# A diffusion backbone step on one core: the down projection's 512 columns as two matmuls of 256, the convolution's tokens divided at 384

## The chip, the cores and the metric

The kernel is one program on one core of a Trainium2 chip. The core has five engines with their own instruction queues: PE (TensorE, matrix products), DVE (VectorE), ACT (ScalarE), POOL (GpSimd) and SP (SyncE, which here only issues DMAs). A matmul has a *stationary* operand, which a weight load (PEld in the profile) puts into the array, and a *moving* operand, whose columns stream past it; the result is written to PSUM, an accumulator memory whose banks hold 512 f32 values in each of 128 partitions. The other working memory is SBUF.

The metric is the device time of one execution in microseconds. Three runs of the kernel before gave 771.39, 771.91 and 772.88 us; the median is 771.91 us.

Two words are used throughout. The *duration* of a matmul is what the profile lists for one instruction; its end is modelled, and durations of neighbouring matmuls overlap. The *pitch* is the time from the start of one matmul to the start of the next one; in a run without gaps the pitch is what a matmul costs.

## The reference

One layer of a hybrid backbone: 128 context tokens and 512 latent tokens, 1024 features each, everything in f32.

```
mod = silu(cond) @ w_ada + b_ada
sh1, sc1, g1, sh2, sc2, g2 = split(mod, 6)
h = rms(x, norm_mix) * (1 + sc1) + sh1
q, k, v, gb, gc, u = split(h @ w_in)              # 512, 128, 128, 512, 512, 512 columns
attn   = attention(rope(rms(q)), rope(rms(k)), v)  # latent: context keys + latent keys
y_conv = gb * conv3(gc * u)                        # 3 taps along the tokens
mix = concat(rms(attn), rms(y_conv)) @ w_out
x = x + g1 * mix
h2 = rms(x, norm_ffn) * (1 + sc2) + sh2
gate, up = split(h2 @ w_gate_up)                   # 2816 columns each
x = x + g2 * ((silu(gate) * up) @ w_down)          # 2816 x 1024
```

The change touches `gb`, `gc` and `u` (the convolution's three projections) and the last product with `w_down`.

## The kernel before, in words

**Split products.** Each f32 operand is split into a high part, rounded to the type fp32r, and a low part, the rest. A product is three matmuls: high by high, high by low, low by high. The helper `mm3` issues them (L155, L156, L157); the convolution has its own three lines (L678, L679, L680). ACT makes the high part of a weight block (L151) and DVE the low part (L152) out of a block `wf` that SP loads; the results are the tiles `wh` and `wl`.

**The stages.** The program goes through the first norm and the queries (to about 61 us of the span), keys and values (61 to 75), attention (75 to 256), the output projection (256 to 325) and then the SwiGLU network (325 to the end). PE's instructions stand in the order in which they are written (a manual schedule); those of DVE and ACT are mostly set by a scheduler with its own cost estimates, and DMAs go through SP's queue.

**Keys and values** (`kv_mm`) take a 128-token slice of `hH` or `hL` (the normed input, features by tokens, high and low) as stationary operand and 256 columns of `wh` or `wl` as moving operand, into the PSUM tile `pc`.

**The convolution** runs the other way: for each of 12 blocks (three projections by four groups of 128 channels) 128 columns of weights are stationary and tokens of `hH` and `hL` move. The 640 tokens are two chunks of 320, each its own accumulator `pc` of 8 contraction tiles by 3 matmuls = 24 matmuls. This is filler work for attention: the generator `conv_mm` yields after k = 2, after k = 5 and at the end, so a chunk is three steps of 9, 9 and 6 matmuls. In the text order of attention (`SEQ`) each `F1` runs one step between a unit's scores (S, L790), transposes (T, L816) and products with the values (O, L833). A finished chunk is evicted by ACT (`gc`, L692) or multiplied by DVE (`u` at L701, `gb` at L713); the table `PIECES` cuts the second chunk where latent and context tokens meet.

**The network** has 22 blocks of 128 hidden columns in four groups of 6, 6, 5 and 5. Gate and up products use moving operands of 320 tokens (half of them) and stationary weights. After each group, `down` multiplies its hidden columns with `w_down`: for both halves j of the 1024 output columns and each of the 5 token tiles, one accumulator `pf` of 512 columns (one PSUM bank) collects, for every hidden block f of the group, three matmuls: a 128-token slice of `gT[f]` (tiles `gH` and `gL`) is stationary and 512 columns of `wh` or `wl` move. In the very last half of the last group the last token tile is halved instead: two accumulators of 256 columns each (`halved`, the variable TL). When an accumulator is done, DVE multiplies it by g2 (L1230) and adds it to x (L1231); in the last group SP then stores it.

Of the kernel before, what the change touches and what calls it, by code (L numbers as in the profile page):

```python
# [15 lines left out]
P = 128  # L16
# [68 lines left out]
AHEAD = 3  # L85
# [6 lines left out]
def build(ctx, tc, x_prompt, x_sample, c, cache_k, cache_v, c_ctx, norm_mix, norm_ffn, w_ada, b_ada,  # L92
# [66 lines left out]
    def rstd_of(ss, n, scale, extra=None, tag="rs"):  # L159
        """(ss * scale + eps) ** -0.5 (times extra)"""  # L160
# [34 lines left out]
    def op_load(e):  # L195
        """one stationary operand of a gate and up block: a quarter of the block, or a sum of quarters"""
        f, name = e[0][1:]
# [120 lines left out]
    def ada1_load(k):  # L318
        """w_ada of feature tile k of the first norm's scale and shift"""
# [51 lines left out]
    # products with the two conditions: four contraction tiles at a time on the four column groups of the  # L371
    # array, each with its conditions in the first columns; the groups' sums are added by sel afterwards
# [12 lines left out]
    def vec_do():  # L385
# [3 lines left out]
        # (1 + b_sc) * norm for both norms  # L389
# [7 lines left out]
    def mod_evict(i, f0, n, ps_sc, ps_sh):  # L397
        """ps_*: [P, n, 2] sums without bias for features f0..f0+n tiles"""
# [35 lines left out]
    def xT_do(t):  # L434
        """the normed tokens of tile t, feature-major"""
# [144 lines left out]
    def head_norm(ps, nh, t, which):  # L580
        """rms over each head, gain, rotary; ps [P, nh*64] -> SBUF f32 [P, nh, 64]"""
# [71 lines left out]
    def q_turn(st):  # L653
        q = T("qT", (P, NH, P), F32R, QTB)
        for g in range(2):
            tp = PB((P, 4, P), F32R)
            for h in range(4):
# [9 lines left out]
    CH = [(0, 320), (320, 320)]  # L667
    # (chunk, columns of the chunk, token columns, columns of the padded row)
    PIECES = [(0, slice(0, 320), slice(0, 320), slice(1, 321)),
              (1, slice(0, 192), slice(320, 512), slice(321, 513)),  # L670
              (1, slice(192, 320), slice(512, 640), slice(515, 643))]

    def conv_mm(off, ct, out):
        wh, wl = W(("conv", off, ct))
        for c0, n in CH:
            acc = PB((P, 320), tag="c")
# [94 lines left out]
    def F(n=1):  # L771
        for _ in range(n):
            if used[0] < NFILL:
                next(filler)
                used[0] += 1

# [1 line left out]
    of = [None] * NT  # L778
    rA = [None] * NT
    qT = [None] * NT  # L780
# [535 lines left out]
```

## Time and profile before

| | |
|---|---|
| median of three runs | 771.91 us (771.39 to 772.88) |
| span of the profiled execution, first to last instruction | 771.6 us; no device time of that execution stands beside it, the median is 0.3 us above the span |
| mean granted clock of TensorE | 0.989 of full speed |
| PE busy | 744.2 us, 96% of the span |
| weight loads (PEld) busy | 669.2 us, 87% |
| DVE, ACT, POOL busy | 563.1 us (73%), 376.8 us (49%), 70.8 us (9%) |
| DMA | 84.53 MB, mean 110 GB/s |
| matmuls of 128x512 in the down projection | 3 x 215 |
| matmuls of 128x256 in its last halved tile | 3 x 10 |
| matmuls of 128x320 in the convolution | 3 x 192 |

How to read the rows: in the timeline a row is start in us, duration in us, engine, source line, operation, output <- inputs by the program's names, the shape and the count. In the table of groups a row is line, engine, operation, names, shape and count, then busy us and mean ns of one, then the engine's idle time before them and what ended it. A row of windows gives a stretch, its length, then each engine's busy us with its number of instructions.

### The profile page before, as it was taken

How to read it: one execution, taken by the hardware profiler on the slowest of the kernel's cores; microseconds unless marked ns; L12 is line 12 of the kernel's file. 1: busy time of each engine (PE TensorE's matmuls, PEld its weight loads, DVE VectorE, ACT ScalarE, POOL GpSimd, SP SyncE). 2: the span in 40 equal slices, each digit the busy share in tenths (PEclk: the TensorE clock that was granted, in tenths of full speed). 3: DMA queues.
4: the chain of work that ended last, by engine and by line, in shares of the span. 5: the costliest groups of instructions: out<-in, count | busy, mean ns of one | idle time of the engine just before them, and what ended most of it. 6: DMA issues, size and time to landing. Idle time of an engine off the chain costs nothing.

```text
span 771.6 us, 11961 instructions
## 1 busy us (share of the span) xinstructions
PE 744.2 (96%) x4580; PEld 669.2 (87%) x4580; DVE 563.1 (73%) x1033; ACT 376.8 (49%) x732; POOL 70.8 (9%) x97
## 2 busy tenths in 40 slices
PE   4999999999999999996999999999999999999997
PEld 3778988989999787886998789999889998899986
DVE  5566887675666799789778777984677866788653
ACT  5446676666665346875452125554125542255510
POOL 3105101011010330044100000000000000000000
PEclk9999999999999999999899999999999999999999
DMA  9984134424325433111134412233112231222312
GB/s 290 308 236 128 42 109 140 121 90 140 120 89 171 161 133 110 56 55 55 56 110 153 134 55 83 83 109 110 54 56 82 83 109 56 80 84 84 110 55 82
DMA packets 102350, 84.53 MB, mean 110 GB/s; under 512 B 4526, under 2 KB 82674, under 8 KB 102292
## 3 DMA queue, kind: packets, MB, share of 16 engines
q1 hardware_dynamic: 100980, 83.39, 35.0%
q8 instruction: 36, 0.59, 0.3%
q10 hardware_dynamic: 1056, 0.26, 0.2%
q0 software_dynamic: 256, 0.11, 0.1%
q14 instruction: 22, 0.18, 0.1%
HBM read 79.68 MB, written 2.75 MB: 107 GB/s over the span
## 4 chain that ended last, share of the span: by engine, by line
PE 83%; DVE 8%; ACT 3%; DMA 2%; issue 2%; SPq 2%; POOL 1%; ACTq 0%; POOLq 0%
PE pf L155 17%; PE pf L157 17%; PE pf L156 17%; PE pc L678 3%; PE pc L679 3%; PE pc L680 3%; PE ps L155 3%; PE ps L156 3%; PE ps L157 3%; PE po L833 2%; PE ps L790 2%; PE pt L816 2%; PE pc L380 2%; DMA af<-in_w_ada_dram 2%; DVE wl L152 1%
## 5 line engine op out<-in xcount | busy, mean ns | idle before, releaser
L151 ACT ACTIVATE wh<-wf 128x1024 fp32r<-128x1024 f32 (+1 forms) x76 | 64.1, 843 | 93.1 <-PE pf L157 63.2
L155 PE MATMUL pf<-wh,gH 128*128 128x512 f32 (+1 forms) x225 | 88.2, 392 | 0.0
L157 PE MATMUL pf<-wh,gL 128*128 128x512 f32 (+1 forms) x225 | 87.7, 390 | 0.0
L156 PE MATMUL pf<-wl,gH 128*128 128x512 f32 (+1 forms) x225 | 87.7, 390 | 0.0
L152 DVE TENSOR_TENSOR wl<-wf,wh 128x1024 fp32r<-128x1024 f32 (+1 forms) x42 | 49.4, 1176 | 27.8 <-ACT wh L151 24.9
L678 PE MATMUL pc<-hH,wh 128*128 128x320 f32 x192 | 61.7, 321 | 0.0
L679 PE MATMUL pc<-hL,wh 128*128 128x320 f32 x192 | 60.0, 312 | 0.0
L680 PE MATMUL pc<-hH,wl 128*128 128x320 f32 x192 | 59.9, 312 | 0.0
L155 PE MATMUL pf<-T,wh 128*128 128x320 f32 x160 | 50.1, 313 | 6.2 <-ACT p L1125 6.2
L155 PEld LDWEIGHTS pf<-wh,gH 128*128 128x128 f32 x225 | 42.3, 188 | 9.8 <-ACT wh L151 0.2
L157 PEld LDWEIGHTS pf<-wh,gL 128*128 128x128 f32 x225 | 42.3, 188 | 9.8
L156 PEld LDWEIGHTS pf<-wl,gH 128*128 128x128 f32 x225 | 42.3, 188 | 9.8 <-issue 0.2
L156 PE MATMUL pf<-T,wh 128*128 128x320 f32 x160 | 49.9, 312 | 0.0
L157 PE MATMUL pf<-T,wh 128*128 128x320 f32 x160 | 49.9, 312 | 0.0
L155 PE MATMUL pf<-T,wl 128*128 128x320 f32 x160 | 49.3, 308 | 0.0
L156 PE MATMUL pf<-T,wl 128*128 128x320 f32 x160 | 49.3, 308 | 0.0
L157 PE MATMUL pf<-T,wl 128*128 128x320 f32 x160 | 49.3, 308 | 0.0
L156 PE MATMUL pf<-B,wl 128*128 128x320 f32 x152 | 47.5, 313 | 0.3 <-DVE B L1020 0.3
L155 PE MATMUL pf<-B,wl 128*128 128x320 f32 x152 | 47.4, 312 | 0.0
L157 PE MATMUL pf<-B,wl 128*128 128x320 f32 x152 | 47.2, 310 | 0.0
L1230 DVE TENSOR_TENSOR dm<-pf,g 128x512 f32<-128x512 f32 (+1 forms) x41 | 27.7, 676 | 22.9 <-PE pf L157 22.9
L151 ACT ACTIVATE wl<-wf 128x512 fp32r<-128x512 f32 x34 | 21.4, 630 | 43.5 <-PE pf L156 36.8
(308 smaller groups left out, 2097.5 us busy)
## 6 DMA issues: line engine op xcount, KB each, us to landing
wf<-in_w_gate_up_dram SPq DMA_DIRECT2D x44, 512.0 KB, 3.8
aw<-in_w_ada_dram SPq DMA_DIRECT2D x24, 512.0 KB, 4.7
wf<-in_w_down_dram SPq DMA_DIRECT2D x20, 512.0 KB, 3.2
wf<-in_w_in_dram SPq DMA_DIRECT2D x18, 512.0 KB, 5.9
af<-in_w_ada_dram SPq DMA_DIRECT2D x32, 256.0 KB, 6.1
x<-in_x_sample_dram SPq DMA_DIRECT2D x8, 512.0 KB, 5.3
wf<-in_w_out_dram SPq DMA_DIRECT2D x8, 512.0 KB, 4.5
wf<-in_w_ada_dram SPq DMA_DIRECT2D x8, 512.0 KB, 3.8
```

The costliest lines, as they stand in the source:

```text
L151: act.activation(hi, src, AF.Copy)
L152: dve.tensor_tensor(lo, src, f32(hi), ALU.subtract)
L155: pe.matmul(out, lh, rh, start=start, stop=False, skip_group_check=more)
L156: pe.matmul(out, lh, rl, start=False, stop=False, skip_group_check=more)
L157: pe.matmul(out, ll, rh, start=False, stop=stop, skip_group_check=more)
L380: pe.matmul(out[CG * g:CG * (g + 1)], cp[:, k], w, start=(k < 4), stop=(k >= KD - 4), skip_group_check=True)
L678: pe.matmul(acc, wh[:, k], hH[k][:, c0:c0 + n], start=(k == 0), stop=False)
L679: pe.matmul(acc, wh[:, k], hL[k][:, c0:c0 + n], start=False, stop=False)
L680: pe.matmul(acc, wl[:, k], hH[k][:, c0:c0 + n], start=False, stop=(k == KD - 1))
L790: pe.matmul(s2[:, g, :320], q, kk[:, v, P + g * 320:P + (g + 1) * 320], start=(i == 0), stop=(i == 1))
L816: pe.transpose(tp[:, i, h], u[3][h][:, kt * P:(kt + 1) * P], ident)
L1230: dve.tensor_tensor(dm, ps[:, :n], g2[cc][:, oc], ALU.mult)
```

## The change

In `down`, the call of `mm3` becomes an explicit loop: the three products of a hidden block are each issued as one matmul per 256 output columns. Both pieces have the same stationary operand, one after the other, and write the two halves of the same PSUM bank. Only the first matmul that touches the bank has the start flag; the second half's first matmul carries none. The halved last tile has one piece of 256 as before, so 645 matmuls of 512 become 1290 of 256, and PE issues 5048 matmuls where it issued 4403 (the profile's 4580 counts some f32 matmuls twice).

In the convolution the chunks become 384 and 256 tokens, `PIECES` follows (384, then 128 latent and 128 context tokens), and the accumulator is a slice of a full bank's tile. The number of matmuls stays; of each pair of 320 one becomes 384 and the other 256.

The rest of the diff takes out comments and docstrings. The lines behind the new loop in `down` move down by five.

```diff
-    CH = [(0, 320), (320, 320)]
-    # (chunk, columns of the chunk, token columns, columns of the padded row)
-    PIECES = [(0, slice(0, 320), slice(0, 320), slice(1, 321)),
-              (1, slice(0, 192), slice(320, 512), slice(321, 513)),
-              (1, slice(192, 320), slice(512, 640), slice(515, 643))]
+    CH = [(0, 384), (384, 256)]
+
+    PIECES = [(0, slice(0, 384), slice(0, 384), slice(1, 385)),
+              (1, slice(0, 128), slice(384, 512), slice(385, 513)),
+              (1, slice(128, 256), slice(512, 640), slice(515, 643))]
...
         for c0, n in CH:
-            acc = PB((P, 320), tag="c")
+            acc = PB((P, 512), tag="c")[:, :n]
...
                 for i, f in enumerate(fs):
-                    mm3(ps[:, :n], gT[f][0][:, s], gT[f][1][:, s], wh[:, i, c0:c0 + n], wl[:, i, c0:c0 + n],
-                        f == grp[0], f == grp[-1])
+                    gh, gl = gT[f][0][:, s], gT[f][1][:, s]
+                    for a, (l, r) in enumerate(((gh, wh), (gh, wl), (gl, wh))):
+                        for c in range(0, n, 256):
+
+                            pe.matmul(ps[:, c:c + 256], l, r[:, i, c0 + c:c0 + c + 256],
+                                      start=f == grp[0] and a == 0 and c == 0, stop=f == grp[-1] and a == 2,
+                                      skip_group_check=True)
```

Two places in PE's built order show it. The first is the start of the down projection of the first group: `pf` is the accumulator of a token tile, `gH` and `gL` are the hidden columns (two blocks here), `wh` and `wl` the weights. The first fence is before, the second after; "x2" means two equal rows in a row.

```order
L155 MATMUL pf_4861<-wh_4799,gH_4207 128x512
L156 MATMUL pf_4861<-wl_4800,gH_4207 128x512
L157 MATMUL pf_4861<-wh_4799,gL_4208 128x512
L155 MATMUL pf_4861<-wh_4799,gH_4321 128x512
L156 MATMUL pf_4861<-wl_4800,gH_4321 128x512
L157 MATMUL pf_4861<-wh_4799,gL_4322 128x512
```

```order
L1219 MATMUL pf_4861<-wh_4799,gH_4207 128x256 x2
L1219 MATMUL pf_4861<-wl_4800,gH_4207 128x256 x2
L1219 MATMUL pf_4861<-wh_4799,gL_4208 128x256 x2
L1219 MATMUL pf_4861<-wh_4799,gH_4321 128x256 x2
L1219 MATMUL pf_4861<-wl_4800,gH_4321 128x256 x2
L1219 MATMUL pf_4861<-wh_4799,gL_4322 128x256 x2
```

Nothing changes place: each row of 512 columns became two of 256 with the same stationary slice and the same bank.

The second is the first filler step of a second chunk of the convolution in attention (`pc` is the chunk's accumulator), the first three of its rows before and after.

```order
L678 MATMUL pc_1166<-hH_34_149,wh_627 128x320
L679 MATMUL pc_1166<-hL_42_157,wh_627 128x320
L680 MATMUL pc_1166<-hH_34_149,wl_628 128x320
```

```order
L678 MATMUL pc_1166<-hH_34_149,wh_627 128x256
L679 MATMUL pc_1166<-hL_42_157,wh_627 128x256
L680 MATMUL pc_1166<-hH_34_149,wl_628 128x256
```

The step keeps its place and its 9 matmuls; it is shorter here, and in the first chunk longer.

## The prediction

> **What bounds the kernel now.** I read the page's sums first, then the chain that ended last, then the groups by shape, then the timeline of PE at four places to get pitches, and last the waits of PE.
>
> ```profile
> PE 744.2 (96%) x4580; PEld 669.2 (87%) x4580; DVE 563.1 (73%) x1033; ACT 376.8 (49%) x732; POOL 70.8 (9%) x97
> ...
> PE 83%; DVE 8%; ACT 3%; DMA 2%; issue 2%; SPq 2%; POOL 1%; ACTq 0%; POOLq 0%
> ```
>
> ```profile
> 436.00:755.00 319.00, 318.98 (x1865) 294.56 (x1864) 230.89 (x370) 126.15 (x226) 0.00 (x0) 1.00 0.26 81
> ```
>
> PE holds 83% of the chain, and in the stretch from 436 to 755 us it is busy without a hole (318.98 of 319.00 us) at the full granted clock, while DVE is busy 230.89 us of it and ACT 126.15. So in the network stage a matmul's pitch is the time: what the down projection's matmuls gain or lose passes to the end. The groups that the change touches, by shape:
>
> ```profile
> L155 PE MATMUL pf<-wh,gH 128*128 128x512 f32 x215 | 85.4, 397 | 0.0
> L157 PE MATMUL pf<-wh,gL 128*128 128x512 f32 x215 | 85.0, 395 | 0.0
> L156 PE MATMUL pf<-wl,gH 128*128 128x512 f32 x215 | 85.0, 395 | 0.0
> ...
> L678 PE MATMUL pc<-hH,wh 128*128 128x320 f32 x192 | 61.7, 321 | 0.0
> ...
> L155 PE MATMUL pc<-wh,hH 128*128 128x256 f32 x40 | 11.4, 285 | 0.0
> ...
> L155 PE MATMUL pf<-wh,gH 128*128 128x256 f32 x10 | 2.8, 277 | 0.0
> ```
>
> The mean durations here (397 for 512 columns, 277 for 256) are longer than the pitches, because rows overlap; two durations of 277 would make 554 against 397, and that would be a wrong way to price the change. The pitch comes from starts in the timeline. First the down projection with 512 columns, then its own halved tile of 256 at the very end:
>
> ```profile
> 560.39 0.39 PE L155 MATMUL pf<-wh,gH 128*128 128x512 f32 x1
> ...
> 572.29 0.39 PE L155 MATMUL pf<-wh,gH 128*128 128x512 f32 x1
> ```
>
> ```profile
> 765.46 0.28 PE L155 MATMUL pf<-wh,gH 128*128 128x256 f32 x1
> ...
> 767.39 0.28 PE L157 MATMUL pf<-wh,gL 128*128 128x256 f32 x1
> ```
>
> Between the first two lie 51 pitches, 11.90 / 51 = 233.3 ns. Between the second two lie 17, 1.93 / 17 = 113.5 ns. So two of 256 take 227.0 ns there and one of 512 takes 233.3. The same form elsewhere, in the keys and values (stage 61 to 75 us) and in attention's products with the values:
>
> ```profile
> 61.70 0.28 PE L155 MATMUL pc<-wh,hH 128*128 128x256 f32 x1
> ...
> 67.28 0.28 PE L157 MATMUL pc<-wh,hL 128*128 128x256 f32 x1
> ```
>
> ```profile
> 110.27 0.28 PE L833 MATMUL po<-ph,VS 128*128 128x256 f32 x1
> ...
> 110.74 0.31 PE L678 MATMUL pc<-hH,wh 128*128 128x320 f32 x1
> ```
>
> There it is 5.58 / 47 = 118.7 ns and 0.47 / 4 = 117.5 ns. The sign of this change hangs on which of the two pitches the new pieces take: they win below 116.65 ns, half of 233.3.
>
> **The change part by part.** *Down projection.* Removed: 645 matmuls of 512 (3 x 215), 645 x 233.3 ns = 150.5 us. Added: 1290 of 256. At 113.5 ns they take 146.4 us, a gain of 4.1 us; at 118.7 ns 153.1 us, a loss of 2.6 us. I take 113.5, because that row is the nearest: same stage, same helper line, same operand tiles (`gH`, `gL` stationary, halves of `wh` and `wl` moving), same kind of bank, with DVE at work beside it, as the chain tells:
>
> ```profile
> 765.66 0.70 DVE dm L1230
> 766.39 0.69 DVE x L1231
> ```
>
> The rows at 118.7 and 117.5 have other tiles at other places of SBUF. What no row shows is a long run of such pieces, two neighbours with the same stationary slice, and writing the halves of a bank in turn. The products with the values come close to the first two: `VS` is stationary twice in turn, and the pitch does not alternate there.
>
> *Weight loads.* 645 more of them, each listed with 188 ns:
>
> ```profile
> L155 PEld LDWEIGHTS pf<-wh,gH 128*128 128x128 f32 x225 | 42.3, 188 | 9.8 <-ACT wh L151 0.2
> ```
>
> In the halved tile they keep up at a pitch of 113.5 ns, so they are hidden behind the matmul before them there. If that cover were short, it would show as the higher pitch already priced.
>
> The page "TensorE: Matmul & The Clock Gate" of the Trainium skill, section "Back-to-back issue gap", speaks against the change: it gives N / 2.4 + 2.5 ns per warm matmul, a fixed cost that is paid once more per piece. As an estimate by that page the 645 further matmuls cost 645 x 2.5 ns = 1.6 us, and the total would be about 773.5. The trace's 233.3 ns at 512 columns, where that rule has 215.8, and 113.5 at 256, where it has 109.2, do not agree with it: here the longer matmul carries more extra time, not the same.
>
> *Convolution.* Removed: 576 matmuls of 320, that is 288 pairs. Added: 288 of 384 and 288 of 256. The pitch at 320, in the convolution and in the network:
>
> ```profile
> 162.93 0.31 PE L678 MATMUL pc<-hH,wh 128*128 128x320 f32 x1
> ...
> 166.46 0.28 PE L833 MATMUL po<-ph,VS 128*128 128x256 f32 x1
> ```
>
> ```profile
> 474.03 0.31 PE L155 MATMUL pf<-T,wl 128*128 128x320 f32 x1
> ...
> 477.99 0.31 PE L155 MATMUL pf<-T,wl 128*128 128x320 f32 x1
> ```
>
> 3.53 / 24 = 147.1 ns and 3.96 / 27 = 146.7 ns. A pair costs 294.2 ns. No row has 384 columns. By the cost per column of the neighbours (113.5 / 256 = 0.443 ns at least, 147.1 / 320 = 0.460 at most) it is 170 to 177 ns; the straight line from 320 to 512 gives 146.7 + 64 x 86.6 / 192 = 175.6. The 256 piece here is between 113.5 and 118.7. So a pair is between 283.5 and 295.7, or -3.1 to +0.4 us over 288 pairs. I take 174.5 + 118 = 292.5 ns, since keys and values use the same `hH`, `hL` and are the nearest 256 row: -0.5 us.
>
> *Evictions of the chunks.* ACT's copy and DVE's products handle the same 640 columns as before, cut at 384; both engines have time there, so nothing.
>
> *The filler's step length.* A step of 9 matmuls in a second chunk falls from 9 x 147.1 = 1.32 us to about 1.06, in a first chunk it rises to 1.57. Attention hides its ACT and DVE work behind these steps. PE's waits between 75 and 256 us are few now:
>
> ```profile
> PE ps L790 <- ACT pr L798: 0.6, 1, 0.6
> PE pt L883 <- ACT wh L151: 0.4, 1, 0.4
> PE pt L658 <- DVE pl L152: 0.2, 1, 0.2
> ```
>
> And this is how close it can be: the exponentials of one unit, the read of their sum, and the scores that reuse the bank after it.
>
> ```profile
> 147.94 0.79 ACT L798 ACTIVATE pr<-ps,nm 128x640 f32<-128x640 f32 x1
> ...
> 148.62 0.20 ACT L798 ACTIVATION_READ_ACCUMULATOR pr<-ps,nm 128x1 f32 x1
> ...
> 148.92 0.39 PE L790 MATMUL ps<-KA,qT 128*128 128x320 f32 x1
> ```
>
> ACT was done at 148.73 to 148.82 and PE came at 148.92, so a step that is 0.26 us shorter would have waited here. The most that this can cost is every shortened step in full: 12 blocks x (2 x 9 + 6) matmuls x (147.1 - 118) ns = 8.4 us. Nothing at all is as possible, and below nothing the three waits, 1.2 us, if longer steps cover them. Since a wait took place at only 3 points in 181 us I take a handful of places of about 0.1 us less what longer steps give back: +0.3 us.
>
> The sum: -4.1 - 0.5 + 0.3 = -4.3 us on the span of 771.6, or 767.3. The median of the runs lies 0.3 us above that span, so the predicted time is 767.6 us, 0.6% faster.
>
> **The rivals.** A time counts as the same within 0.2% (1.5 us), about what a measurement of this kernel can tell from no change.
>
> *The pieces take the higher pitch (other side).* If a run of 256 pieces costs 118.7 ns as in the keys and values, the down projection loses 2.6 us, the convolution's pair is 175.6 + 118.7 = 294.3 (nothing), and with +0.3 the time is 771.9 + 2.9 = 774.8 us. A milder form is a straight line through 320 and 512: (233.3 - 146.7) / 192 = 0.451 ns per column and 2.3 ns per matmul, so 256 costs 117.8, the loss is 645 x 2.3 = 1.5 us, and the time 773.7. It decides from 116.65 ns up. For it speak two stages with three kinds of operands; against it the halved tile, which is the very code that is now repeated.
>
> *The gain is given back after each group.* If DVE's and ACT's preparation of the next group's weights were paced by their own work, PE would arrive 0.5 us earlier at each of the seven later phases and wait there. The time would be 771.9 - 0.5 + 0.3, about 771.7. For it: DVE is 72% busy in 436 to 755. Against it: PE had no hole in that stretch, so the preparation ran ahead.
>
> *Short steps expose attention.* If a third of the bound above is paid, 2.8 us in place of 0.3, the time is 770.1; if all of it is, 775.7.
>
> *The throttle.* After its longest wait PE runs slower for a while:
>
> ```profile
> 366.08 0.64 PE L155 MATMUL pf<-T,wh 128*128 128x320 f32 x1 [6.16 <-ACT p L1125]
> 366.51 0.47 PE L156 MATMUL pf<-T,wh 128*128 128x320 f32 x1
> 366.78 0.47 PE L157 MATMUL pf<-T,wh 128*128 128x320 f32 x1
> ```
>
> The pitch is 270 ns there, nearly twice the 147 of the same shape. A shift of 1 us can move such a phase, either way, by some tenths; the three runs differ by 1.5 us already. It widens the range and is no case of its own.
>
> **How the numbers follow.** The forecast (pitch near 113.5, little lost in attention) has 0.65; its own range is 765.0 to 769.5, from a convolution at its best (-3.1) with a throttle phase the wrong way, to a pitch of 115 in the down projection (645 x 3.3 ns = 2.1 us of gain). The higher pitch has 0.20, of which the milder form, still the border of the same, takes 0.07. The gain given back has 0.07, attention 0.08 (0.04 faster, 0.02 same, 0.02 slower). Faster: 0.65 + 0.04 = 0.69, cut to 0.67 for a mild throttle loss; slower: 0.13 + 0.02 = 0.15, with the same allowance 0.16; the same: the remaining 0.17. The range of 765.0 to 773.6 leaves out the strong form of the higher pitch (0.13), a full loss in attention (0.02) and a little below.
>
> **What would show it.** Right: in the down projection the pitch of the new 256 rows is 113 to 114 ns throughout, also in the middle of the run, where two neighbours share `gH`, and a group's phase at 560 us is shorter by 3%. The convolution's 384 rows have a pitch of 173 to 176 ns, its 256 rows 114 to 119. PE's waits in attention stay below 2 us. Wrong: a pitch above 116.65 ns in the down projection, above all one that alternates between the two pieces of one stationary slice; waits of PE on ACT or DVE in the network after each down phase; or a list of waits in attention that has many places of 0.2 us after short steps.

## The result: 0.5% slower, where 0.6% faster was forecast

| kernel | executions | median, lowest to highest, us | ratio of the medians |
|---|---|---|---|
| before | 20 | 772.27 (769.89 to 775.43) | |
| after | 20 | 776.28 (771.07 to 778.55) | 1.0048, 95% interval 1.0033 to 1.0062 |

The time is outside the range on record (765.0 to 773.6). In all executions here the device time is 1.8 us above the span, so the profile of before (span 771.6) is of an execution of about 773.4 us, 1.1 us above its median.

The profile that came with the 20 executions is of the quickest of them (span 769.3, time 771.07). A later profile of the same kernel (e11 below, span 774.2, time 776.06) lies at the median. Both are shown, because their difference is half of what there is to learn. First the page of the quick one: sums, and the chain that ended last.

```profile
PE 741.1 (96%) x5225; PEld 694.0 (90%) x5225; DVE 563.8 (73%) x1033; ACT 376.5 (49%) x732; POOL 72.0 (9%) x97
...
PE 82%; DVE 8%; ACT 3%; DMA 2%; SPq 2%; issue 2%; POOL 1%; ACTq 0%; POOLq 0%
```

The 645 further matmuls are there (4580 to 5225), with as many weight loads. PE's share is what it was, so the sums don't tell where the time is. Windows by stage do. The three rows are: the first latent scores of attention (L790; the context tokens' part, from 74 us, lies ahead of it) to the first matmul of the output projection; from there to the first down matmul; from there to the end. After the length come PE's, PEld's, DVE's, ACT's and POOL's busy us, then the granted clock, the DMA share and GB/s. Before:

```profile
93.49:256.18 162.69, 161.96 (x1178) 146.93 (x1176) 113.71 (x227) 102.57 (x208) 11.75 (x23) 1.00 0.37 119
256.18:414.44 158.26, 148.82 (x840) 134.12 (x839) 133.11 (x232) 89.28 (x185) 36.66 (x33) 0.97 0.30 97
414.44:771.63 357.19, 353.21 (x2025) 322.47 (x2023) 256.50 (x410) 131.13 (x231) 0.00 (x0) 1.00 0.28 86
```

After, the quick execution:

```profile
93.65:259.49 165.84, 163.18 (x1178) 147.13 (x1177) 114.12 (x228) 102.12 (x209) 11.68 (x23) 1.00 0.37 116
259.49:415.57 156.08, 147.62 (x840) 132.85 (x839) 133.54 (x231) 89.56 (x186) 37.82 (x33) 0.98 0.31 98
415.57:769.29 353.72, 349.74 (x2670) 348.32 (x2668) 256.63 (x410) 131.11 (x231) 0.00 (x0) 1.00 0.28 87
```

After, the execution at the median (e11):

```profile
93.70:259.34 165.64, 162.99 (x1177) 147.12 (x1176) 114.14 (x228) 102.15 (x209) 11.69 (x23) 1.00 0.37 117
259.34:416.38 157.04, 147.67 (x840) 132.80 (x839) 133.44 (x231) 89.52 (x186) 37.79 (x33) 0.98 0.31 97
416.38:774.25 357.87, 353.96 (x2670) 352.54 (x2668) 257.28 (x410) 131.22 (x231) 0.00 (x0) 1.00 0.28 86
```

Three things are to be seen. Attention is about 3 us longer in both (165.84 and 165.64 against 162.69). The network from the first down matmul is 3.5 us shorter in the quick execution and 0.7 us *longer* in the other, by the same instructions. The stage between them has nothing that was changed; it took 158.26 us at a granted clock of 0.97, and 156.08 and 157.04 us at 0.98.

Attention first. PE's waits in 75 to 256 us of the kernel before were three, 1.2 us. After, for 75 to 260 us:

```profile
PE ps L790 <- DVE KB L625: 1.1, 1, 1.1
PE pt L816 <- DVE pl L152: 0.7, 1, 0.7
PE po L833 <- DVE pl L152: 0.4, 1, 0.4
PE pt L883 <- ACT wh L151: 0.4, 1, 0.4
PE ps L790 <- ACT pr L798: 0.3, 1, 0.3
```

The first three wait for DVE, and none of these three stood in the list before. The largest, on DVE's own timeline (start, duration, line, operation): before, the two casts of `KB` (keys of the second head, for the scores) stand close together, and the split of a weight block, 1.22 us long, comes after them.

```profile
92.55 0.42 DVE L625 CAST KB<-pt 128x256 fp32r<-128x256 f32 x1
93.00 0.17 DVE L167 TENSOR_SCALAR rs<-rs 128x8 f32<-128x8 f32 x1
93.08 0.42 DVE L625 CAST KB<-pt 128x256 fp32r<-128x256 f32 x1
...
94.08 1.22 DVE L152 TENSOR_TENSOR wl<-wf,wh 128x1024 fp32r<-128x1024 f32 x1
```

After, the weight split stands between them, and PE shows what that does:

```profile
92.72 0.42 DVE L625 CAST KB<-pt 128x256 fp32r<-128x256 f32 x1
...
93.58 1.22 DVE L152 TENSOR_TENSOR wl<-wf,wh 128x1024 fp32r<-128x1024 f32 x1
94.71 0.42 DVE L152 TENSOR_TENSOR m<-of,m 128x256 fp32r<-128x256 f32 x1
95.05 0.42 DVE L625 CAST KB<-pt 128x256 fp32r<-128x256 f32 x1
```

```profile
94.09 0.31 PE L790 MATMUL ps<-KB,qT 128*128 128x320 f32 x1
95.52 0.41 PE L790 MATMUL ps<-KB,qT 128*128 128x320 f32 x1 [1.12 <-DVE KB L625]
```

The two scores start 1.43 us apart, where their pitch is 0.15: 1.3 us are lost at this one place. It is not that PE came early behind a shorter step: its first scores start at 93.65 us, before at 93.49, but the second cast ends at 95.47, before at 93.50. Neither cast nor weight split was edited. That the scheduler changed the order because the chunks have other estimated lengths is the likely reason; e5 below bears on it.

The convolution's own matmuls cost what they did. In the timeline of after, a first chunk and a second chunk:

```profile
100.14 0.34 PE L679 MATMUL pc<-hL,wh 128*128 128x384 f32 x1
...
101.37 0.34 PE L680 MATMUL pc<-hH,wl 128*128 128x384 f32 x1
```

```profile
95.89 0.28 PE L679 MATMUL pc<-hL,wh 128*128 128x256 f32 x1
...
96.36 0.29 PE L680 MATMUL pc<-hH,wl 128*128 128x256 f32 x1
```

1.23 / 7 = 175.7 ns and 0.47 / 4 = 117.5 ns, a pair 293.2 and before 294.2, in these rows. Over all 288 pairs of the kernel with the convolution's part alone (e2), the starts of its matmuls, compared one by one with those of before, give +0.1 us. In this are two places where a wait behind a chunk went away (0.5 us); the matmuls alone cost about 0.6 us more, with means of 176.6 and 119.8 ns, together 296.4 against 294.0 of before counted in the same way.

Now the down projection. The new groups, and the window whose row was shown of before, have no hole:

```profile
L1219 PE MATMUL pf<-wh,gH 128*128 128x256 f32 x440 | 87.2, 278 | 0.0
...
L1219 PEld LDWEIGHTS pf<-wh,gH 128*128 128x128 f32 x440 | 66.9, 188 | 0.5 <-ACT wh L151 0.2 <-issue 0.2
```

```profile
436.00:755.00 319.00, 318.98 (x2407) 317.76 (x2407) 232.33 (x372) 127.38 (x227) 0.00 (x0) 1.00 0.26 81
```

PE has work for 318.98 of 319.00 us, as before, so the pitch is the time. In the second group's phase of the quick execution:

```profile
539.92 0.39 PE L1219 MATMUL pf<-wh,gH 128*128 128x256 f32 x2
...
569.84 0.39 PE L1219 MATMUL pf<-wh,gH 128*128 128x256 f32 x2
```

and of the execution at the median:

```profile
539.82 0.40 PE L1219 MATMUL pf<-wl,gH 128*128 128x256 f32 x2
...
569.97 0.40 PE L1219 MATMUL pf<-wh,gH 128*128 128x256 f32 x2
```

29.92 us hold 264 pitches, 113.3 ns; 30.15 us hold 256, 117.8 ns. The instructions, operands and granted clock (1.00) are the same. Two pieces of 256 take 226.7 or 235.6 ns where one of 512 took 233.3: a gain or a loss.

### The profile page after: what moved, and what is told of

Its sections match the earlier page's. It is cut to its first block, busy times and chain, and to the rows that moved or that the text cites. A ratio compares the mean times of both kernels' runs of the same rounds, so it can differ in the third digit from the quotient of the medians.

```text
span 769.3 us, 13252 instructions
## 1 busy us (share of the span) xinstructions
PE 741.1 (96%) x5225; PEld 694.0 (90%) x5225; DVE 563.8 (73%) x1033; ACT 376.5 (49%) x732; POOL 72.0 (9%) x97
## 4 chain that ended last, share of the span: by engine, by line
PE 82%; DVE 8%; ACT 3%; DMA 2%; SPq 2%; issue 2%; POOL 1%; ACTq 0%; POOLq 0%
PE pf L1219 19%; PE pf L155 11%; PE pf L156 11%; PE pf L157 11%; PE pc L678 3%; PE pc L679 3%; PE pc L680 3%; PE ps L155 3%; PE ps L156 3%; PE ps L157 3%; PE po L833 2%; PE ps L790 2%; PE pt L816 2%; DMA af<-in_w_ada_dram 2%; PE pc L380 2%
## 5 line engine op out<-in xcount | busy, mean ns | idle before, releaser
L1219 PE MATMUL pf<-wh,gH 128*128 128x256 f32 x440 | 87.2, 278 | 0.0
L1219 PE MATMUL pf<-wl,gH 128*128 128x256 f32 x440 | 86.8, 277 | 0.0
L1219 PE MATMUL pf<-wh,gL 128*128 128x256 f32 x440 | 86.8, 277 | 0.0
L152 DVE TENSOR_TENSOR wl<-wf,wh 128x1024 fp32r<-128x1024 f32 (+1 forms) x42 | 49.3, 1174 | 27.9 <-ACT wh L151 24.8
L1219 PEld LDWEIGHTS pf<-wh,gH 128*128 128x128 f32 x440 | 66.9, 188 | 0.5 <-ACT wh L151 0.2
L1219 PEld LDWEIGHTS pf<-wh,gL 128*128 128x128 f32 x440 | 66.8, 188 | 0.0
L1219 PEld LDWEIGHTS pf<-wl,gH 128*128 128x128 f32 x440 | 66.8, 188 | 0.0
L678 PE MATMUL pc<-hH,wh 128*128 128x384 f32 (+1 forms) x192 | 61.8, 322 | 0.0
L679 PE MATMUL pc<-hL,wh 128*128 128x384 f32 (+1 forms) x192 | 59.8, 312 | 0.0
L680 PE MATMUL pc<-hH,wl 128*128 128x384 f32 (+1 forms) x192 | 59.7, 311 | 0.0
L155 PE MATMUL pf<-T,wh 128*128 128x320 f32 x160 | 50.0, 313 | 5.1 <-ACT p L1125 5.1
L156 PE MATMUL pf<-T,wh 128*128 128x320 f32 x160 | 49.8, 311 | 0.0
L155 PE MATMUL pf<-T,wl 128*128 128x320 f32 x160 | 49.2, 308 | 0.0
L156 PE MATMUL pf<-T,wl 128*128 128x320 f32 x160 | 49.2, 308 | 0.0
L156 PE MATMUL pf<-B,wl 128*128 128x320 f32 x152 | 47.0, 309 | 0.3 <-DVE B L1020 0.3
L155 PE MATMUL pf<-B,wl 128*128 128x320 f32 x152 | 46.9, 308 | 0.0
L155 PE MATMUL pf<-B,wh 128*128 128x320 f32 x136 | 42.0, 309 | 0.0
```

Of the source, the lines that this page charges most:

```text
L152: dve.tensor_tensor(lo, src, f32(hi), ALU.subtract)
L155: pe.matmul(out, lh, rh, start=start, stop=False, skip_group_check=more)
L156: pe.matmul(out, lh, rl, start=False, stop=False, skip_group_check=more)
L678: pe.matmul(acc, wh[:, k], hH[k][:, c0:c0 + n], start=(k == 0), stop=False)
L679: pe.matmul(acc, wh[:, k], hL[k][:, c0:c0 + n], start=False, stop=False)
L680: pe.matmul(acc, wl[:, k], hH[k][:, c0:c0 + n], start=False, stop=(k == KD - 1))
```

## The experiments

Where the table gives no ratio, there was one execution only. "Attention" is from the first latent scores to the output projection, "network" from the first down matmul to the end, both from the profiled execution. Before has 162.69 and 357.19 us.

| run | median, lowest to highest, us (executions) | ratio, 95% interval | attention | network |
|---|---|---|---|---|
| e1 down only | 770.06, 765.96 to 773.73 (12) | 0.9971, 0.9948 to 0.9993 | 162.99 | 353.72 |
| e2 convolution only | 776.43, 773.49 to 779.16 (11) | 1.0048, 1.0033 to 1.0064 | 165.74 | 357.17 |
| e3 after again | 773.69, 768.88 to 777.32 (12) | 1.0020, 0.9998 to 1.0042 | 166.22 | 352.93 |
| e4 convolution 256, 384 | 775.21, 772.86 to 778.00 (9) | 1.0041, 1.0026 to 1.0056 | 164.73 | 357.18 |
| e5 convolution, first block 320 | 773.73, 771.66 to 777.60 (12) | 1.0028, 1.0012 to 1.0044 | 164.67 | 357.15 |
| e6 halves apart | 769.33, 765.88 to 774.47 (12) | 0.9975, 0.9956 to 0.9995 | 162.65 | 352.92 |
| e7 aligned | 770.52, 766.87 to 772.91 (12) | 0.9981, 0.9962 to 1.0000 | 162.32 | 353.72 |
| e8 down only | 773.01 | | 162.94 | 357.08 |
| e9 down only | 773.37 | | 163.08 | 357.86 |
| e10 down only | 767.41 | | 163.01 | 352.93 |
| e11 after | 776.06 | | 165.64 | 357.87 |
| e12 down, marker | 774.11, 771.09 to 775.63 (8) | 1.0039, 1.0026 to 1.0051 | 163.04 | 358.60 |
| e13 after, marker | 775.82, 775.48 to 777.31 (5) | 1.0060, 1.0046 to 1.0074 | 165.78 | 358.60 |
| e14 down, long marker | 775.95, 774.48 to 778.81 (10) | 1.0054, 1.0036 to 1.0072 | 163.20 | 360.83 |
| e15 down, first product whole | 771.08, 769.21 to 772.47 (12) | 0.9982, 0.9968 to 0.9997 | 162.81 | 355.48 |
| e16 down, marker and whole product | 771.46, 767.51 to 775.54 (12) | 0.9995, 0.9976 to 1.0015 | 162.97 | 353.64 |
| e17 down, two markers | 772.12, 768.74 to 775.79 (12) | 1.0001, 0.9981 to 1.0021 | 163.07 | 354.92 |
| e18 as e16 | 767.53 | | 162.63 | 353.64 |

### The two parts apart, and the whole again

e1 has only the loop in `down`, e2 only `CH`, `PIECES` and the accumulator, e3 is the changed kernel once more.

> Only the down projection's split, the convolution stays at 320 and 320. Theory A (the split pays and the loss of the whole change comes from the convolution's chunks in attention): a pitch of 113.3 ns in the down projection and 4.1 us faster than the kernel before, a ratio near 0.995. Rival B (the loss comes with the 645 further matmuls, for instance by instruction loading or by the rest of the network waiting): a ratio of 1.000 or more, with PE waits or holes between 415 us and the end.

> Only the convolution's chunks of 384 and 256, the down projection stays at 512. Theory A: attention (75 to 256 us) grows by 3 us as in the changed kernel's profile, or by up to 8 us in other executions, a ratio of 1.004 to 1.010. Rival B: attention costs nothing on the average, a ratio within 0.002 of 1.

> The changed kernel itself, for a second profile: the one at hand is of an execution of 771.07 us, the fastest of 20, where the median is 776.28. Theory A: a profile of a common execution has 113.3 ns in the down projection too, and some 7 to 8 us more than the kernel before in attention. Rival B: attention is as in the first profile and the missing 5 us lie elsewhere, in the network or in half-clock stretches.

The down projection's part alone makes the kernel 0.3% faster, the convolution's part alone makes it 0.5% slower, and it is the convolution's part that lengthens attention: 165.74 us in e2, 162.99 in e1. In all 13 profiles with the convolution as before this stage takes 162.3 to 163.2 us, in all five with 384 and 256 tokens 165.6 to 166.2. PE's list of waits in e2 begins with the three rows shown of after, with the same figures. A wait costs a little more than its row says (1.3 for the 1.1), so I compared the starts of PE's instructions in e2 and before one by one: +1.5 us around the `KB` wait at 93.8 us, +0.65 at 104.1 and +0.7 at 131.3 of the kernel before; many smaller gains and losses add 0.2, together the 3.05 us between the two stages. At the two later places DVE's order had changed as well. The wait at 104.1 is for a split `pl` (L152): in e2 the product `qT` (L650, 0.68 us) and a scaling (L805) stand ahead of it on DVE, before they stood behind it. The one at 131.3 is for another such split, which in e2 stands behind a weight split of 1.22 us and before stood ahead of it.

The whole, run again, came out at 1.0020 and not at 1.0048, and its profile has the shortest network of the three (352.93). The 7 to 8 us in attention that theory A named for it were not there (166.22, 3.5 more than before). So the size was not settled by these three: e1 gained 2.4 us where theory A had 4.1, and the first half of its first down phase ran at 117.8 ns.

### Is it DVE's order or the short steps?

e4 turns the chunks round, so that the first is the short one. e5 leaves the first of the 12 convolution blocks at 320 and 320 and changes the other eleven, which brings back the order of DVE around the `KB` casts.

```diff
 e4
-    CH = [(0, 384), (384, 256)]
+    CH = [(0, 256), (256, 384)]
 e5
+    def chunks(off, ct):
+        return [(0, 320), (320, 320)] if (off, ct) == (O_GC, 0) else CH
...
-        for c0, n in CH:
+        for c0, n in chunks(off, ct):
```

> As the run with the convolution alone, but the chunks in the other order, 256 and then 384 tokens. The same matmuls, and the step between the last keys' transposes and the first scores is now a long one. Theory A (the loss is a few places where a short step and a changed order on DVE uncover a wait): PE's wait on the KB copy near 95 us is gone and the stage of attention is 0 to 2 us longer than before, not 3, a ratio of 1.000 to 1.003. Rival B (the chunk sizes themselves cost it): 3 us longer again, a ratio near 1.005.

> As the run with the convolution alone, but the first of the 12 blocks keeps chunks of 320 and 320; with it DVE copies KB ahead of the weight block's low part again. Theory A: the wait on KB at 95 us (1.1 us and 0.4 around it) is gone, so about half of the loss in attention comes back, and the ratio is near 1.002. Rival B (a loss spread over all blocks): a twelfth comes back, a ratio near 1.0045.

In e5 the casts stand together again and the `KB` wait is gone, and with it 1.1 of the 3.05 us of attention (164.67 against 165.74); a third came back, between the half of theory A and the twelfth of rival B. The ratio falls from 1.0048 to 1.0028, though the two intervals overlap. So the loss at 93.8 us comes from DVE's order there and not from the chunk sizes in general, since eleven blocks still have them; the steps around that place were changed back together with the order. e4 lost the `KB` wait too, and its attention (164.73) is as long as that of e5, but its ratio (1.0041) can't be told from that of e2. Its list of waits is a new one:

```profile
PE ps L790 <- ACT pr L798: 1.3, 2, 1.0
PE pt L658 <- ACT qT L659: 0.7, 1, 0.7
PE pt L658 <- DVE pl L152: 0.5, 1, 0.5
```

Attention is again 2 us longer than before. Each new set of lengths came with another list of waits. Whether the 2 us that remain in e5 and in e4 are order as well, or the shorter steps, was not separated.

### What sets the pitch? Operands and addresses

e6 issues the three products of the first 256 columns before those of the second, so that a slice of `gH` stands twice in turn instead of four times, and one of `gL` once instead of twice. It does not take the repeats away: the products high by high and high by low still share their slice. e7 puts a pad of 32 bytes per partition ahead of `hH` and `hL`, which moves them to multiples of 64 bytes (a memset of the pad on POOL comes with it).

```diff
 e6
-                    for a, (l, r) in enumerate(((gh, wh), (gh, wl), (gl, wh))):
-                        for c in range(0, n, 256):
+                    for c in range(0, n, 256):
+                        for a, (l, r) in enumerate(((gh, wh), (gh, wl), (gl, wh))):
 e7
+    pad = T("pad", (P, 8))
+    pool.memset(pad, 0.0)
```

> Only the down projection's split, and for each hidden block the three products of the first 256 columns come before the three of the second, so that three neighbours in a row no longer repeat a stationary slice as pairs do. Theory P (a run of 256 pieces has two steady pitches, 113.3 and 117.8 ns, and an execution falls into one or the other by the moment at which the run begins): both pitches can be found again, the times spread over 8 us and the ratio lies between 0.993 and 1.000. Rival Q (the higher pitch comes from the repeated slice): 113.3 ns in all four phases, a narrow spread and a ratio of 0.9945.

> Only the down projection's split, and a tile of 32 bytes is added ahead of the tiles hH and hL, so that they begin at multiples of 64 bytes in each partition, as gH and gL do, and not 32 bytes beside. Theory R (the pitch of 118.7 ns in keys and values comes from that place): keys and values run at 113 to 114 ns, the convolution at 146.7 in place of 147.1, 0.6 us and 0.2 us less. Rival S (place has nothing to do with it, the higher pitch is the other of two steady states): 117 to 119 ns as before.

e6's ratio is about that of e1. Its one profile has 113.3 ns in all phases, as Q said, but its times spread over 8.6 us and its ratio is not the 0.9945 of Q. Against Q speaks rather that phases with the slice four times in turn run at 113.3 in most profiles; a run without any repeat was not made. In e7 the keys and values changed from a pitch that scattered between 115 and 122 (mean 118.7) to an even 117.8 for the first 48 pieces. The pieces behind a gap of 1.7 us then ran at 113.3: the same two pitches, one run each, outside the down projection. The convolution's 320 columns went from 147.0 to 146.7. The first half of the first down phase ran at 117.8 as well. So with the tiles at multiples of 64 bytes the scatter was gone, in this one profile, and both pitches stayed.

### More executions of the same two kernels

> The down split alone again, for one more profiled execution of it; nothing is left out. Theory P (two steady pitches): executions of this kernel differ because 256-column pieces run at 113.3 or at 117.8 ns through whole unbroken stretches, and the length of the network stage, from the first down matmul to the end, follows the count of pieces at the higher pitch: 353 us with none of the 1290 there, 354 with the first half of the first phase there (as once measured), 359 with all. Theory Q (the spread lies elsewhere, in the half-speed stretches of the clock or in attention): the network stage stays at 353 to 354 us whatever the total, and no piece outside the first phase runs at 117.8. An execution below 769 us says nothing against either.

> The same kernel once more, with the same expectations: under P the network stage (353 us at best) is longer by 4.5 ns for each piece at the higher pitch, and a total of 773 us comes with some 800 or more of the 1290 pieces there; under Q a total of 773 us comes with a network stage of 353 to 354 us.

> The same kernel once more, with the same expectations: under P the network stage (353 us at best) is longer by 4.5 ns for each piece at the higher pitch, under Q it stays at 353 to 354 us.

> The changed kernel a third time, for one more profiled execution; nothing is left out. Under P its network stage is 353 us plus 4.5 ns for each of the 1290 pieces at 117.8 ns, and a total of 776 us, its median so far, comes with a stage of 357 us or more. Under Q the stage stays at 353 to 354 us and a total of 776 us comes from attention, above the 3.3 us that it lost in the two profiles so far. Under both the first scores come within 1 us of 94 us and the output projection's start is 2.5 to 4 us later than the 256.2 us of before.

This decides for theory P against Q. In the nine profiles whose phases begin as in after (after, e1, e3, e6 to e11) the network stage takes only four values, and they follow from which phases ran at which pitch:

| pieces at 117.8 ns | network, us | profiles |
|---|---|---|
| none | 352.9 | e3, e6, e10 |
| first half of the first phase | 353.7 | after, e1, e7 |
| phases 2, 3 and 4 | 357.1 | e8 |
| both | 357.9 | e9, e11 |

By the pitch difference of 4.45 ns, the 180 pieces of the first half phase give 0.8 us and the 960 of phases 2 to 4 give 4.3: the four values to 0.2 us. Before has 357.2. So the split gains 4.3 us, or loses 0.7, with steps between. Within a phase the pitch never changes by itself. The second half of the first phase, which begins behind the two f32 products of L999, was at 113.3 in all nine.

There is a sign at the entry. Of e10 and of e9, the last three gate and up matmuls and the first two pairs of pieces of the third phase:

```profile
631.58 0.31 PE L156 MATMUL pf<-B,wh 128*128 128x320 f32 x1
631.72 0.30 PE L157 MATMUL pf<-B,wh 128*128 128x320 f32 x1
631.87 0.40 PE L1218 MATMUL pf<-wh,gH 128*128 128x256 f32 x2
632.10 0.40 PE L1218 MATMUL pf<-wl,gH 128*128 128x256 f32 x2
632.34 0.39 PE L1218 MATMUL pf<-wh,gL 128*128 128x256 f32 x2
```

```profile
634.90 0.31 PE L156 MATMUL pf<-B,wh 128*128 128x320 f32 x1
635.04 0.31 PE L157 MATMUL pf<-B,wh 128*128 128x320 f32 x1
635.19 0.40 PE L1218 MATMUL pf<-wh,gH 128*128 128x256 f32 x2
635.43 0.40 PE L1218 MATMUL pf<-wl,gH 128*128 128x256 f32 x2
635.66 0.40 PE L1218 MATMUL pf<-wh,gL 128*128 128x256 f32 x2
```

To the nanosecond, the last matmul of 320 has a pitch of 141 to 143 ns where the pieces then run at 113.3, and of 144 or 145 where they run at 117.8: at all 36 entries of the nine profiles (22 and 14). So the choice seems to be made before the first piece, by something that lives on in the stretch of 320 columns. What that is no run shows.

The listed weight loads differ too. In the nine profiles every third load of a stretch at 117.8 ns takes about 192 ns in place of 187 or 188 (60 of 180 loads in the first half phase, 120 of 360 in the second phase). In a stretch at 113.3 ns there is at most one such load. Whether that is the cause or another sign stays open.

### What stands ahead of the pieces

e12 and e13 put one f32 matmul of 64 columns, a marker whose result is not read, ahead of each down phase: e12 in the kernel of e1, e13 in the changed kernel. e14 makes the marker 512 columns long. e15 has no marker, but leaves the first product of each phase whole.

```diff
 e12, e13 (in down, ahead of the loop over j)
+        pe.matmul(PB()[:, :64], ones, ones[:, :64], start=True, stop=True)
 e14
+        pe.matmul(PB(), ones, g2[0][:, :512], start=True, stop=True)
 e15
-                        for c in range(0, n, 256):
+                        w = n if f == grp[0] and j == 0 and t == 0 and a == 0 else 256
+                        for c in range(0, n, w):
```

> The down split alone, plus one f32 matmul of 64 columns of ones, whose result nobody reads, at the start of each of the four down phases. In all nine profiles of split kernels so far the pieces behind the f32 matmuls of L999 ran at 113.3 ns, whatever the pitch before. Theory F (an f32 matmul puts the pieces behind it into the lower pitch): all four phases run at 113.3 to 113.6 ns, the network stage is 353 us plus 0.2 to 0.5 us for each of the four added matmuls, 354 to 355 us, and the upper end of the times falls: a median of 767.5 to 769 us, none above 771.5, a ratio of 0.993 to 0.996. Theory G (any interruption draws the pitch anew): phases at 117.8 ns remain, the times still reach from 766 to 774 us, and the median is that of the down split alone or 1 us above, a ratio of 0.997 to 0.999.

> The changed kernel with the same four added matmuls. Under F its network stage is 354 to 355 us as well, and with the 3.2 us that the convolution's part loses in attention its median is 770.5 to 772.5 us, a ratio of 0.998 to 1.000: the down projection's gain and attention's loss then nearly cancel. Under G the median stays between 774 and 777 us, a ratio of 1.002 to 1.006.

> The down split alone with one f32 matmul of 512 columns (of g2, into a bank that nobody reads) at the start of each of the four down phases, where the run before had 64 columns of ones. Theory H (what stands right ahead sets the pitch: short f32 passes of 57 and 83 ns put the pieces into 117.8 ns, long ones of 429 ns, as at L999, into 113.3): all four phases at 113.3 to 113.6 ns, a network stage of 353 us plus about 0.9 us for each marker, 356 to 357 us, and close times: a median of 769.5 to 771.5 us and no execution above 773, a ratio of 0.997 to 1.000. Theory K (any added f32 matmul in front of a phase leads to 117.8 ns): the phases at 117.8 again, a stage of 361 to 362 us, a median of 775 to 778 us, a ratio of 1.004 to 1.008.

> The down split alone, but the very first product of each of the four phases stays one matmul of 512 columns; no marker. If a long matmul of the same type ahead of the pieces already sets 113.3 ns (the strong form of H), all phases are at 113.3, the network stage is 353 us, and the times lie close together: a median of 766 to 768.5 us, none above 771, a ratio of 0.992 to 0.996. If it needs the f32 passes, the pitch is drawn as before: executions from 766 to 774 us, a ratio of 0.996 to 0.999. If one ordinary long matmul puts the pieces into 117.8, the median is 773 to 775 us and the ratio 1.001 to 1.004.

Both theories failed in e12: the marker did settle the pitch, but at 117.8 ns, at all four entries of e12 and all four of e13, whose median then is the one that G had named, for another reason. The network of 358.60 us is the 357.9 of "both" plus 0.7 for three markers within it. H fell with e14: a marker of 512 columns, as long as L999's, leads to 117.8 too, at four entries of four, and K comes nearest (network 360.83). As far as the profiles go these kernels are the split with the high pitch held on in all but half a phase. They are slower than before, by 0.4 to 0.6%, but not from the pitch alone: e13 has the convolution's loss in it, and e14's markers cost 1.0 us each.

e15 is nearest to the second of its three expectations, but not by a free draw. Two phases ran at 113.3 and two at 117.8, and the sign at the entry had turned round: a last pitch of 145 led to 113.3, one of 141 or 142 to 117.8, at four of four. The third phase of e15:

```profile
630.99 0.30 PE L157 MATMUL pf<-B,wh 128*128 128x320 f32 x1
631.13 0.39 PE L1219 MATMUL pf<-wh,gH 128*128 128x512 f32 x1
631.36 0.40 PE L1219 MATMUL pf<-wl,gH 128*128 128x256 f32 x2
631.60 0.40 PE L1219 MATMUL pf<-wh,gL 128*128 128x256 f32 x2
```

By this, one matmul more or less ahead of the pieces turns the pitch over. That suggested putting both together (e16: marker, then the whole product), and two markers one behind the other (e17), as the two f32 products of L999 stand.

> The down split alone with both: the f32 marker of 64 columns at the start of each of the four phases, and then the very first product whole, as one matmul of 512 columns. The marker alone put all pieces into 117.8 ns; the whole product alone turned the result over (an entry that led to 117.8 without it led to 113.3 with it, and the reverse, at four of four entries). Theory M (the marker fixes the starting point, and one single matmul ahead of the pieces turns the pitch over): all four phases at 113.3 ns in every execution, a network stage of 354 to 355 us, a median of 767 to 769.5 us, none above 772, a ratio of 0.993 to 0.997. Theory K (behind a marker the pitch is 117.8 whatever follows): a stage of 359 to 360 us, a median of 773 to 776 us, a ratio of 1.002 to 1.006.

> The down split alone with two f32 markers of 64 columns at each phase's start, one behind the other, and no whole product. At L999, where two f32 products stand one behind the other, the pieces always ran at 113.3 ns. If the number of f32 products turns the pitch over (M in its wider form), all phases are at 113.3, the network stage is 354.5 to 355.5 us, the median 767.5 to 770 us, the ratio 0.994 to 0.998. If the passes count (two for each product, always an even number), all phases are at 117.8 as with one marker, the median is 774 to 777 us and the ratio 1.003 to 1.007.

> The kernel with marker and whole product once more, since its times reached from 767.5 to 775.5 us although its one profile had all four phases at 113.3 ns. If M holds, all phases are at 113.3 ns again, the network stage is 353.5 to 354.5 us, and a total above 772 us would come from the stages ahead of it, with a first down matmul after 416.5 us. If the marker doesn't fix the starting point in every execution, some phases run at 117.8, and the network stage is longer by up to 4.5 ns for each such piece, 1.6 us for a phase of 360.

In the three profiles all twelve phases run at 113.3 ns. The third phase of e16:

```profile
633.51 0.33 PE L1198 MATMUL pt<-ones 128*128 128x64 f32 x2
633.64 0.48 PE L1220 MATMUL pf<-wh,gH 128*128 128x512 f32 x1
633.96 0.39 PE L1220 MATMUL pf<-wl,gH 128*128 128x256 f32 x2
634.19 0.39 PE L1220 MATMUL pf<-wh,gL 128*128 128x256 f32 x2
```

So in every profile the number of f32 products or whole matmuls ahead of the pieces went with the pitch once a marker stood there: one marker gives 117.8, one marker and one whole product 113.3, two markers 113.3. But the times did not fall as M said. e16's reach from 767.5 to 775.5 us, and its median is that of before. Both its profiles are of executions in the lower half (769.47 and 767.53), so they can't tell whether the others had phases at 117.8 or lost their time ahead of the network. The clock that each execution lists is a hint: at 0.989 four executions of e16 took 770.55 to 775.54 us, seven of before, over the sessions of the experiments, 772.16 to 773.17. That speaks against the throttle alone and for phases at 117.8 in the slower executions; no profile shows them. This stays open, and with it whether the pieces can be held at 113.3. The best kernel that was measured is the down projection's part alone (e1, and e6 with nearly the same ratio): 0.3% faster than before, with intervals that end just below 1.

## Why the prediction was wrong

**What bounds the kernel** was read rightly: PE has no hole in the network stage, and each nanosecond of pitch went to the end. That the gain is *given back after each group* was not seen in any profile.

**The down projection, -4.1 us.** The mechanism and the size are right where the pieces run at 113.3 ns: -4.3 us. The first step that failed is "I take 113.5, because that row is the nearest". It gave one pitch to one place. The prediction had both pitches in its rows, 113.5 and 117.5 to 118.7, and took them as two forecasts of which one would come true; in fact the same instructions take either, by the execution and by the phase. Phases 2 to 4 ran at 117.8 in 3 of 9 profiles, the first half phase in 5 of 9. By that share the term is -4.3 + 4.3 x 3/9 + 0.8 x 5/9 = -2.4 us, and e1's median is 2.4 us below that of before in its session (772.42); with nine profiles so close an agreement is partly luck. The prediction also says that no row shows two neighbours with the same stationary slice. The halved tile does: its L155 and L156 both load `gH`. The border of 116.65 ns was right, and the rival of the higher pitch came true in part: +0.7 us for the stage where all but half a phase has it, against the 1.5 to 2.6 on record, as half of the first phase stays low.

**The weight loads** leave no hole on PE at either pitch: the list shows each load starting 2 to 5 ns behind a matmul's start in both. The prediction's "if that cover were short, it would show as the higher pitch" is not ruled out: at 117.8 every third load is listed as 4 ns longer.

**The page's fixed cost.** The section "Back-to-back issue gap" of "TensorE: Matmul & The Clock Gate" in the Trainium skill gives N / 2.4 + 2.5 ns for what it calls the isolated matmul, so 2.5 ns more for each further one. At the higher pitch the trace agrees with the sign and nearly with the size of that difference: 2 x 117.8 - 233.3 = 2.3 ns. At the lower one it does not: 2 x 113.3 - 233.3 = -6.7 ns.

**The convolution's matmuls, -0.5 us**, were about +0.6 us in e2: a pair costs 176.6 + 119.8 = 296.4 ns on the average, above the 295.7 that the prediction had as its highest. That is a miss of about 1 us, and it is part of what attention lost.

**Evictions "so nothing", and +0.3 us for attention.** This is the second step that failed, and the term that was furthest off: attention cost 3.0 to 3.5 us in all profiles with the changed convolution. The prediction looked for steps that would no longer cover work on ACT. The three largest losses, together about 2.9 us, are waits for DVE at places where its instructions stand in another order. The largest, 1.3 us, is at a place where DVE had been done 0.3 us early before; e5 took that one back, the other two were not tested one by one. The front's part on the change shows PE's order alone, where indeed nothing moves; I did not set DVE's beside it, though the text says that a scheduler sets it. The rival "short steps expose attention" had the right size (2.8 us), by another cause than the one found at the largest place, and 0.08 was too little for it.

**The throttle.** The stage between attention and the first down matmul took 154.8 to 158.6 us in the 20 profiles, without any change in it, at mean granted clocks of 0.99 to 0.96. That is more than the "some tenths" of the prediction. The quick profile of after has this stage 2.2 us shorter than the profile of before, and would have misled alone.

**The sum.** +3.0 to +3.5 for attention and -4.3 to +0.7 for the network give -1.3 to +4.2 us against before; the two measurements of the changed kernel were +4.0 and +1.3 (773.69 against 772.42 in e3's session). Neither miss alone explains that: with the forecast's -4.1 an attention of +3.1 leaves the kernel faster, and with the convolution untouched e1 was faster than before at the pitches that came. Together they give a slower one. That the first 20 executions had mostly the high pitch fits the third profile, which has it in all but half a phase and lies at the median; for the others there is no profile, so this part is inferred.

## What to carry to other kernels

Where a scheduler sets an engine's order from estimated lengths, a change of a tile's size can change that order: set the orders of *all* engines side by side before pricing a stage at "a little", above all around the places where a wait ends with little to spare. Where the rows of one shape show two pitches in two stages, expect that the new code may take either, and price their mixture. And one profile is one execution: here the one that came first was the quickest of twenty, and only one near the median showed what the median is made of.

## What the runs showed of the hardware that was not expected

Matmuls of 256 columns, each with a weight load of its own, run at one of two even pitches, 113.3 or 117.8 ns, at full granted clock and with the same operands. The choice stands at the entry of an unbroken run and is kept through its 180 to 360 matmuls. In the runs of 512 columns only one pitch was seen (233.3 ns), and 320 columns show it at most as 141 to 143 against 144 or 145 ns in the very last matmul ahead of the pieces. One whole matmul ahead turned the meaning of that sign round (4 of 4 entries in e15); behind f32 products the pitch was the same in every profile of a kernel (24 of 24 entries in e12 to e14 and e16 to e18): 117.8 behind one, 113.3 behind two or behind one and a whole matmul. At 117.8 every third weight load is listed with 192 ns in place of 187 or 188. The cause itself stays open.
